# A chunked linear-recurrence scan laid out on 64x64 tiles of the array, with the solve's product in the bank of the state sum

## The chip, the cores and the metric

The kernel runs on one core of a Trainium2 chip. The metric is the device time of one execution in microseconds. Everything is fp32; on TensorE an fp32 matmul is two instructions in the trace (fp32r products aside).

## The reference

Two layers run over two batches with the same weights: a prompt of 256 tokens and a sample of 1024, 1280 tokens of width 1024 in all. Layer 0 mixes tokens by RWKV-7 in both directions, layer 1 by neighbourhood attention; each is followed by a squared-ReLU MLP. The change is in layer 0, whose core is this recurrence for 16 heads of 64, once forwards and once backwards:

```python
    def step(S, inp):
        r_t, w_t, k_t, v_t, a_t, b_t = inp
        sa = jnp.einsum('bhvk,bhk->bhv', S, a_t)
        S = S * w_t[:, :, None, :] + sa[..., None] * b_t[:, :, None, :] + v_t[..., None] * k_t[:, :, None, :]
        return S, jnp.einsum('bhvk,bhk->bhv', S, r_t)
...
        y = y + _wkv_scan(rf, _heads(decay), k_d, vf, -kk, kk * iclr, reverse=(d == 1))
        bonus = bonus + jnp.sum(rf * k_d * r_k, axis=-1, keepdims=True)
...
    y = ((y - mu) * lax.rsqrt(var + GN_EPS)).reshape(B, T, C) * lnx_g + lnx_b
    y = y + (bonus * vf).reshape(B, T, C)
```

## The kernel before

Tokens go in chunks of L = 64; heads go in pairs, m = 0 to 7, two heads filling P = 128 partitions (e = 0, 1 for the upper and lower 64). Within a chunk the recurrence is closed with a triangular system, so that each chunk is some matrix products with the 64x64 state S of each head.

**Stages.** The projections and LoRA products come first; then the operands of the scan are prepared per head pair and direction (`prep_open` and what follows it) and stored to DRAM as `ar_d` (a and r) and `bk_d` (b and k), and the bonus sums r*k_d*r_k are taken with one matmul per 128 tokens (L699, bps). Then the scan, the output projection, the MLP, attention and the second MLP.

**The scan** is ten jobs of 16 chunk steps and two directions: job 0 and 1 take the prompt (four head pairs with four chunks each), jobs 2 to 9 one head pair of the sample. The order of instructions on PE, DVE (VectorE), ACT (ScalarE) and POOL is written out by hand: `at(t, f)` gives each piece a time in steps, and the pieces are issued in the order of those times (`scan_until`); each engine runs its instructions in that order. DMA issues are SyncE's and ACT's.

A job's side work is spread over the steps before and beside it. In each of eight groups (direction d, four chunks) there are: `prod`, the product of b and a, r (L812, aps), masked into zb by DVE (L814); its store, and the reload as `mt` for the triangular solves, which DVE does in 31 pairs of rank-one operations (L857, L859) on 32x32 blocks; `merge1` and `merge2`, which join two 32-blocks with 32x32 matmuls (L903, L921) and two ACT copies; `kprod`, k with a, r (L953, kps), copied by ACT (L956) and masked by POOL (L958) into zk; `ktr`, the transpose of b, k (L967, lps, L970) into lt. PSUM tiles of these come from rotating buffers with the tag aps.

**A step** (`scan_step`) is one direction of one chunk, for both heads of the pair in 128x128 tiles with zeros off the diagonal: s0 w = zk times v (L1012); s1 adds S times ar (L1023) and ACT copies two 64x64 parts to u (L1027); s2 the solve, us = Q times u (L1032), copied by ACT to hv (L1034) and u2 (L1041); s3 the state sum, us = lt times hv (L1046), and DVE's update S = us*D + sd (L1054), where sd = S*D is POOL's (L1016); s4 w += zb times u2 (L1060), whose lower half is the chunk's y, copied by ACT (L1063) or added by DVE (L1065). The two directions are half a step apart.

`scan_post` normalises y per job in two halves (L1116 to L1163), transposes it (L1168) and stores it to z_d.

Of the kernel before, what the change touches and what calls it, by code (L numbers as in the profile page):

```python
# [23 lines left out]
NEG = -1e30  # L24
L2_EPS = 1e-24
# [3 lines left out]
V_QG, V_KG = 136, 137  # L29
NVEC = 138  # L30
# [18 lines left out]
class Trunk:  # L49
    def __init__(self, ctx, tc, a):  # L50
# [16 lines left out]
        self.dall = self.cp.tile([P, 8, 2, 20], F32, name="dall")  # L67
        self.bonus = self.cp.tile([P, 10, NH], F32, name="bonus")
# [33 lines left out]
    def l0_proj(self):  # L102
# [10 lines left out]
        W = 1283  # L113

# [400 lines left out]
    def prep_open(self, bctx):  # L515
        nc, tc, a = self.nc, self.tc, self.a
        self.ar_d = self.dram("ar_d", [8, 2, P, 20, P])
        self.bk_d = self.dram("bk_d", [8, 2, P, 20, P])
# [117 lines left out]
    def prep_products(self, U, h, i):  # L636
# [7 lines left out]
        if "ar" not in u:  # L644
            for nm in ("ar", "bk"):
                u[nm] = pk.tile([P, 8, P], F32, name=nm, tag=nm)
            u["kd"] = pk.tile([P, 512], F32, name="kd", tag=f"kd{d}", bufs=2)
            u["st"] = [(self.ar_d[m, d, :, ch0:ch0 + nch, :], u["ar"][:, :nch, :]), (self.bk_d[m, d, :, ch0:ch0 + nch, :], u["bk"][:, :nch, :])]
        ar, bk, kd = u["ar"], u["bk"], u["kd"][:, :w]
        if i == 0:  # L650
            nc.vector.tensor_tensor(out=ar[:, :nch, 64:128], in0=c3(r), in1=ec[:, :nch, 1 - d:65 - d], op=ALU.mult)
# [4 lines left out]
        elif i == 3:  # L656
            nc.vector.tensor_tensor(out=bk[:, :nch, 64:128], in0=c3(kd), in1=emc, op=ALU.mult)
        elif i == 4:
            nc.vector.scalar_tensor_tensor(out=tha, in0=tha, scalar=1.0, in1=kk, op0=ALU.add, op1=ALU.mult)
        elif i == 5:  # L660
            nc.vector.scalar_tensor_tensor(out=ar[:, :nch, 0:64], in0=c3(kk), scalar=-1.0, in1=ec[:, :nch, d:64 + d], op0=ALU.mult, op1=ALU.mult)
        elif i == 6:
            nc.vector.scalar_tensor_tensor(out=bk[:, :nch, 0:64], in0=c3(tha), scalar=0.5, in1=emc, op0=ALU.mult, op1=ALU.mult)
# [25 lines left out]
    def prep_bonus(self, U, h, step):  # L689
# [6 lines left out]
        elif step == 1:  # L696
            u["pb"] = self.ppn.tile([P, 8], F32, name="bps", tag="bps")
            for b in range(nb):
                nc.tensor.matmul(u["pb"][:, 2 * b:2 * b + 2], u["kd"][:, b * P:(b + 1) * P], self.blk, start=True, stop=True)  # L699
        else:  # L700
            nc.vector.tensor_copy(self.bonus[:, c0 // P:c0 // P + nb, 2 * m:2 * m + 2], u["pb"][:, :2 * nb].rearrange("p (b h) -> p b h", h=2))
# [6 lines left out]
    def scan_begin(self):  # L708
# [8 lines left out]
        self.r_hv, self.r_v2, self.r_q = ([[er.tile(shape, F32, name=name + "0")], 0] for name, shape in  # L717
                                          (("hv", [P, 16, P]), ("v2", [P, 16, P]), ("qq", [P, 16, 2, 64])))
        self.r_bb, self.r_ar, self.r_zb = ([[er.tile([P, 4, P], F32, name=f"{name}{i}") for i in range(n)], 0] for name, n in
                                           (("bb", 3), ("ar", 10), ("zb", 10)))  # L720
        for t in self.r_bb[0]:
            nc.gpsimd.memset(t, 0.0)
# [17 lines left out]
    def scan(self):  # L740
        nc, tc, pool = self.nc, self.tc, self.spool
        rp = self.rp = pool("rp", 1)
        fx = pool("fx", 1)

        def grow(r, pl, name, shape, n=1):
            r[0] += [pl.tile(shape, F32, name=f"{name}{len(r[0]) + i}") for i in range(n)]
        grow(self.r_hv, fx, "hv", [P, 16, P])
        grow(self.r_v2, fx, "v2", [P, 16, P])
        grow(self.r_q, fx, "qq", [P, 16, 2, 64])
        grow(self.r_ar, rp, "ar", [P, 4, P], 10)  # L750
        grow(self.r_zb, rp, "zb", [P, 4, P], 10)
        self.r_bk, self.r_u2, self.r_u1, self.r_s = [[], 0], [[], 0], [[], 0], [[], 0]
        grow(self.r_bk, fx, "bdk", [P, 4, P], 2)
        self.sp = pool("sp", 4)
# [3 lines left out]
        self.pbank = [self.pw.tile([P, 2, P], F32, name=f"us{d}") for d in range(2)]  # L758
        for r, nm, n in ((self.r_u2, "u2", 4), (self.r_u1, "u1", 3), (self.r_s, "S", 4)):
            grow(r, fx, nm, [P, P], n)  # L760
        for r in (self.r_bk, self.r_v2, self.r_u2, self.r_u1, self.r_s, self.r_q):
            for t in r[0]:
                nc.gpsimd.memset(t, 0.0)
# [13 lines left out]
    def scan_job(self, j):  # L777
# [4 lines left out]
        J = {"ar": {}, "zb": {}, "zk": {}, "lt": {}}  # L782
        order = [(0, 0), (1, 3), (0, 1), (1, 2), (0, 2), (1, 1), (0, 3), (1, 0)]


        T0 = -34.0

        def first(J=J):
            J["dd"] = [self.dsc.tile([16, 2, 64, 64], F32, name="dd", tag="dd") for _ in range(2)]
        at(T0, first, min(j + 1, 3))  # L790
        for n, (d, g) in enumerate(order):
            m, c0 = grp[g]
            t = T0 + 2 * n
            E = 1 if j == 0 else 2 if j == 1 and n < 2 else 3

            def load(d=d, g=g, m=m, c0=c0):
                ar = self.nxt(self.r_ar)
                nc.sync.dma_start(ar, self.ar_d[m, d, :, c0:c0 + 4, :])
                bb = self.nxt(self.r_bb)
                for e in range(2):  # L800
                    es = slice(64 * e, 64 * e + 64)
                    nc.sync.dma_start(bb[es, :, es], self.bk_d[m, d, es, c0:c0 + 4, 0:64])
                J["ar"][d, g], J["bb", d, g] = ar, bb

            def prod(c, d=d, g=g):
                ar, bb = J["ar"][d, g], J["bb", d, g]
                if c == 0:
                    J["zb"][d, g] = self.nxt(self.r_zb)
                    J["pa"] = self.pa.tile([P, 4, P], F32, name="aps", tag="aps")
                ps = J["pa"]  # L810
                if c < 4:
                    nc.tensor.matmul(ps[:, c, :], bb[:, c, :], ar[:, c, :], start=True, stop=True)  # L812
                if c == 4:
                    nc.vector.tensor_tensor(out=J["zb"][d, g], in0=ps, in1=self.mask[d].unsqueeze(1).to_broadcast([P, 4, P]), op=ALU.mult)  # L814

            def store(d=d, g=g, j=j):
                nc.sync.dma_start(J["dd"][d].rearrange("c e s t -> (e s) c t")[:, 4 * g:4 * g + 4, :], J["zb"][d, g][:, :, 0:64])
            at(t - (2.4 if j else 5.0), load, E)
            for c, dt in enumerate((0.05, 0.07, 0.22, 0.25, 0.38)):
                at(t + dt, lambda c=c, f=prod: f(c), E)  # L820
            at(t + 1.0, store, E)


        T1 = T0 + (15.2 if j else 16.13)

# [11 lines left out]
        at(T1, mload, 1 if j == 0 else 3)  # L837
# [4 lines left out]
        for i in range(4):  # L842
            at(T1 + (1.6 + 0.17 * i if j else 0.912 + 0.1 * i), lambda i=i: mtr(i), 1 if j == 0 else 3)
        T2 = T1 + (2.77 if j else 2.359)
        T3, load = T2, 0.0
        for jj in range(31, 0, -1):
# [13 lines left out]
            at(T3, rank1, 1 if j == 0 else 3)  # L860
            load += 400 + 2 * jj * (32 - jj)
            if load > 877.08:
# [11 lines left out]
        for i in range(4):  # L874
            at(T3 + (0.17 if j else 0.1) * i, lambda i=i: qst(i), 1 if j == 0 else 3)

        def qld():
            Q = self.nxt(self.r_q)
            qx = self.rp.tile([P, 16, 32], F32, name="qx", tag="qx", bufs=2)
            J["Q"], J["qx"] = Q, qx  # L880
# [1080 lines left out]
```

## Time and profile before

| | us |
|---|---|
| median of 3 runs | 4312.45 (4303.99 to 4316.88) |
| the profiled execution | 4314.01 |
| its span | 4312.1 |
| scan loop, 768.6 to 1565 | 796.4 |
| PE busy over the span | 3991.1 (93%) |
| DVE busy | 2660.7 (62%) |
| ACT busy | 1813.1 (42%) |
| POOL busy | 1426.1 (33%) |

Busy times are from one profiled execution. A row of a group of instructions reads: line, engine, operation, output tile<-inputs, for a matmul the rows*columns of the array that it uses, shapes, count | busy us, mean ns of one | idle time of the engine before them, and what ended it. PEld is the load of the weights, which overlaps PE. A row of a stretch of time gives its length, the busy time and count of PE, PEld, DVE, ACT and POOL, then the clock granted to PE (1.00 is full), the busy share of the DMA engines and GB/s. A row of the timeline begins with the start and the length.

### The profile page before, as it was taken

Reading aid. Unit: us, or ns where it says so; the run is one execution under the profiler, and the core shown is the slowest. Engines: PE = TensorE matmul, PEld = TensorE weight load, DVE = VectorE, ACT = ScalarE, POOL = GpSimd, SP = SyncE. Lnnn points to the kernel's source line nnn. Section 1 sums busy time; section 2 is a strip of 40 time slices with the busy share of each in tenths; the row PEclk is TensorE's granted clock in tenths of the full one; section 3 lists DMA queues with packets and bytes.
Section 4 is the critical chain, followed back from the end, with each engine's and each line's share of the span. In section 5 each row is a group of like instructions: output and inputs, shape, how many; then the busy total and the mean of one; then the engine's idle time right before and its main releaser. Section 6 shows DMA issues by size and latency. Waiting matters only on the chain.

```text
span 4312.1 us, 69598 instructions
## 1 busy us (share of the span) xinstructions
PE 3991.1 (93%) x25060; PEld 3342.6 (78%) x25060; DVE 2660.7 (62%) x5390; ACT 1813.1 (42%) x4803; POOL 1426.1 (33%) x1498
## 2 busy tenths in 40 slices
PE   7888878888998879999999998999998999999999
PEld 4665668777777758888888888877676888888888
DVE  7889963577787654755555555166665655555555
ACT  6766641677777753111111123355554311111111
POOL 5440001234444443422222234144444432222222
PEclk9997879899999989999999999999998999999999
DMA  3335565566666434111111104333335211111111
GB/s 120 81 107 198 196 201 144 141 157 155 153 151 153 108 97 133 38 39 36 40 35 40 40 31 152 117 72 77 78 70 161 65 40 40 40 35 39 35 40 59
DMA packets 484537, 400.25 MB, mean 93 GB/s; under 512 B 289216, under 2 KB 392864, under 8 KB 484192
## 3 DMA queue, kind: packets, MB, share of 16 engines
q1 hardware_dynamic: 447968, 328.56, 28.1%
q10 hardware_dynamic: 34416, 61.35, 3.9%
q0 software_dynamic: 1808, 5.90, 0.4%
q8 instruction: 197, 3.23, 0.3%
q14 instruction: 148, 1.21, 0.1%
HBM read 285.66 MB, written 121.24 MB: 94 GB/s over the span
## 4 chain that ended last, share of the span: by engine, by line
PE 69%; DVE 14%; ACT 6%; DMA 5%; issue 4%; POOL 2%; SPq 1%; ACTq 0%; DVEq 0%; POOLq 0%
PE ps L97 17%; PE ps L99 16%; PE ps L98 16%; PE w L1060 2%; PE us L1032 2%; PE kps L953 1%; PE aps L812 1%; PE vps L503 1%; PE vps L505 1%; PE vps L504 1%; PE op L1876 1%; PE us L1046 1%; PE w L1012 1%; DVE S L1054 1%; ACT u L1041 1%
## 5 line engine op out<-in xcount | busy, mean ns | idle before, releaser
L1433 DVE TENSOR_TENSOR x<-ps,x 128x256 f32<-128x256 f32 x1488 | 814.1, 595 | 628.3 <-PE ps L99 628.0
L97 PE MATMUL ps<-ah,whi 128*128 128x512 f32 (+1 forms) x2304 | 843.1, 366 | 5.0 <-ACT whi L91 4.2
L99 PE MATMUL ps<-ah,wlo 128*128 128x512 f32 (+1 forms) x2304 | 824.0, 358 | 2.1 <-POOL wlo L92 2.0
L98 PE MATMUL ps<-al,whi 128*128 128x512 f32 (+1 forms) x2304 | 823.5, 357 | 2.6 <-POOL al L1323 2.6
L92 POOL TENSOR_TENSOR wlo<-raw,whi 128x1024 fp32r<-128x1024 f32 (+1 forms) x178 | 390.5, 2194 | 851.9 <-ACT whi L91 807.8
L97 PE MATMUL ps<-hh,whi 128*128 128x512 f32 (+1 forms) x1536 | 546.9, 356 | 13.8 <-DVE x L1433 13.8
L99 PE MATMUL ps<-hh,wlo 128*128 128x512 f32 (+1 forms) x1536 | 545.9, 355 | 0.0
L98 PE MATMUL ps<-hl,whi 128*128 128x512 f32 (+1 forms) x1536 | 545.2, 355 | 0.0
L97 PEld LDWEIGHTS ps<-ah,whi 128*128 128x128 f32 x2304 | 438.8, 190 | 80.2 <-issue 13.1
L91 ACT CAST whi<-raw 128x1024 fp32r<-128x1024 f32 (+1 forms) x206 | 200.7, 975 | 696.5 <-PE ps L98 630.6
L99 PEld LDWEIGHTS ps<-ah,wlo 128*128 128x128 f32 x2304 | 437.8, 190 | 67.8 <-POOL wlo L92 2.9
L98 PEld LDWEIGHTS ps<-al,whi 128*128 128x128 f32 x2304 | 438.5, 190 | 63.0 <-POOL al L1323 2.9
L1412 POOL TENSOR_TENSOR rl<-rl 128x512 f32<-128x512 f32 (+1 forms) x192 | 174.3, 908 | 500.6 <-PE ps L99 458.3
L97 PEld LDWEIGHTS ps<-hh,whi 128*128 128x128 f32 x1536 | 291.4, 190 | 57.4 <-DVE x L1433 16.8
L1411 ACT ACTIVATE rl<-ps 128x512 f32<-128x512 f32 (+1 forms) x192 | 100.8, 525 | 546.4 <-PE ps L99 546.4
L98 PEld LDWEIGHTS ps<-hl,whi 128*128 128x128 f32 x1536 | 291.4, 190 | 41.0
L99 PEld LDWEIGHTS ps<-hh,wlo 128*128 128x128 f32 x1536 | 291.4, 190 | 41.1
L1414 ACT CAST hh<-rl 128x512 fp32r<-128x512 f32 (+1 forms) x192 | 105.5, 549 | 321.0 <-POOL rl L1412 320.9
L1054 DVE SCALAR_TENSOR_TENSOR S<-us,dall,sd 64x64 f32<-64x64 f32 x512 | 145.0, 283 | 126.4 <-PE us L1046 115.7
L1415 DVE TENSOR_TENSOR hl<-rl,hh 128x512 fp32r<-128x512 f32 (+1 forms) x192 | 119.4, 622 | 151.6 <-ACT hh L1414 151.1
L1016 POOL TENSOR_TENSOR sd<-S,dall 128x128 f32<-128x128 f32 x256 | 122.5, 480 | 258.2 <-DVE S L1054 174.8
L1060 PE MATMUL w<-u,zb 128*128 128x128 f32 x640 | 158.2, 330 | 47.0 <-ACT u L1041 44.8
(310 smaller groups left out, 8222.4 us busy)
## 6 DMA issues: line engine op xcount, KB each, us to landing
raw<-in_w_down_dram SPq DMA_DIRECT2D x64, 512.0 KB, 3.5
raw<-in_w_up_dram SPq DMA_DIRECT2D x64, 512.0 KB, 3.4
ar<-ar_d SPq DMA_DIRECT2D x80, 256.0 KB, 3.4
bk<-bk_d SPq DMA_DIRECT2D x80, 256.0 KB, 3.5
ar_d<-ar ACTq DMA_DIRECT2D x32, 512.0 KB, 2.7
bk_d<-bk ACTq DMA_DIRECT2D x32, 512.0 KB
bs<-tab SPq DMA_DIRECT2D x128, 96.0 KB, 3.9
v_d<-vt ACTq DMA_DIRECT2D x80, 128.0 KB, 4.0
```

The costliest lines, as they stand in the source:

```text
L91: nc.scalar.copy(hi[:, cs], raw)
L92: lo_eng.tensor_tensor(out=lo[:, cs], in0=raw, in1=hi[:, cs].bitcast(F32), op=ALU.subtract)
L97: mm(ps, sh, mh, start=first, stop=False)
L98: mm(ps, sh, ml, start=False, stop=False)
L99: mm(ps, sl, mh, start=False, stop=last)
L1016: nc.gpsimd.tensor_tensor(out=R["sd"], in0=st["S"], in1=self.dall[:, m, d, ch:ch + 1].to_broadcast([P, P]), op=ALU.mult)
L1054: nc.vector.scalar_tensor_tensor(out=S2[es, es], in0=sn[es, es], scalar=D, in1=R["sd"][es, es], op0=ALU.mult, op1=ALU.add)
L1060: nc.tensor.matmul(w, J["zb"][d, g][:, c, :], R["u2"], start=False, stop=True, skip_group_check=True)
L1412: nc.gpsimd.tensor_tensor(out=r[:, :n], in0=r[:, :n], in1=r[:, :n], op=ALU.mult)
L1414: nc.scalar.copy(hh[:, :n], r[:, :n])
L1415: nc.vector.tensor_tensor(out=hl[:, :n], in0=r[:, :n], in1=hh[:, :n].bitcast(F32), op=ALU.subtract)
L1433: nc.vector.tensor_tensor(out=xv, in0=ps[:, :n], in1=xv, op=ALU.add)
```

## The change

All products of the scan are written on 64x64 tiles of the array. HALVES names the two pairs of partition halves: a matmul with the operands on es (64 rows) and the output on es or eo (64 columns) is one tile, so that a product of both heads is two matmuls on different tiles, and a, r, b, k and v lie in tiles of 64 columns without zeros off the diagonal. Both directions are one chain: one set of ACT copies per step serves both. The state sum is in PSUM as identity times S, plus lk times v, plus lb times u, and ACT scales it by the decay when it copies it back; DVE's update and POOL's sd are gone. The banks are b_a (for w's first half), two b_y and two b_s; U, the solve's product, is in columns 128 to 255 of the b_s bank whose first 128 columns take the state sum. Three rotating buffers (pa) serve the side work, where DVE masks zk straight from PSUM. The output transposes and `ktr` are matmuls with the identity. Operands are stored in DRAM by kind and token, the affine part of the normalisation goes to an ACT activation after the transpose, and the bonus sums become 64x64 matmuls per chunk and head. The budget of rank-one work per half step goes from 877.08 to 930.

```diff
+HALVES = ((slice(0, 64), slice(64, 128)), (slice(64, 128), slice(0, 64)))
...
-            for b in range(nb):
-                nc.tensor.matmul(u["pb"][:, 2 * b:2 * b + 2], u["kd"][:, b * P:(b + 1) * P], self.blk, start=True, stop=True)
+            for c in range(2 * nb):
+                for es, eo in HALVES:
+                    nc.tensor.matmul(u["pb"][eo, c:c + 1], u["kd"][es, c * L:(c + 1) * L], self.one[es], start=True, stop=True)
...
+        self.b_a = self.pw.tile([P, 512], F32, name="ba")
+        self.b_y, self.b_s = ([self.pw.tile([P, 512], F32, name=f"{nm}{i}") for i in range(2)] for nm in ("by", "bs"))
...
+            def prod(h, d=d, g=g):
+                if h == 0:
+                    J["pa"] = w4(self.pa.tile([P, 512], F32, name="aps", tag="aps"))
+                if h < 2:
+                    for c in (2 * h, 2 * h + 1):
+                        for es, eo in HALVES:
+                            mm(J["pa"][es, c], J["bb", d, g][es, c], J["aa", d, g][es, c], start=True, stop=True)
...
-            if load > 877.08:
+            if load > 930.0:
                 T3, load = T3 + 0.5, 0.0
...
+            def kprod(h, d=d, g=g):
...
+                    for c in (2 * h, 2 * h + 1):
+                        for es, eo in HALVES:
+                            mm(J["pb"][es, c], bb[es, c], rr[es, c], start=True, stop=True)
+                            mm(J["pk"][eo, c, 0:64], kk[es, c], aa[es, c], start=True, stop=True)
+                        for es, eo in HALVES:
+                            mm(J["pk"][eo, c, 64:128], kk[es, c], rr[es, c], start=True, stop=True)
+                elif h == 2:
+                    zk = J["zk", d, g] = self.rp.tile([P, 4, P], F32, name="zk", tag="zk", bufs=5)
+                    nc.vector.tensor_tensor(out=zk, in0=J["pk"], in1=b4(self.mask[d], P), op=ALU.mult)
...
         def s0():
+            A, Y, sn, U = banks()
+            for d, g, c, cc, m, ch in dirs:
+                zk, v, yd = J["zk", d, g], J["v"], 1 - d if second else d
+                for es, eo in HALVES:
+                    mm(A[es, d], zk[eo, c, 0:64], v[eo, cc], d == 0, new)
+                    mm(Y[eo, yd], zk[eo, c, 64:128], v[eo, cc], d == 0, False)
+                if not end:
+                    for es, eo in HALVES:
+                        mm(sn[es, d], J["lk", d, g][eo, c], v[eo, cc], d == 0, False)
...
+            for d, g, c, cc, m, ch in dirs:
+                yd = 1 - d if second else d
+                for es, eo in HALVES:
+                    mm(A[es, d], J["aa", d, g][es, c], S[es, d], False, True)
+                    mm(Y[eo, yd], J["rr", d, g][es, c], S[es, d], False, False)
+            if not end:
+                for d in range(2):
+                    for es, eo in HALVES:
+                        mm(sn[es, d], self.ident[es, es], S[es, d], False, False)
+
+        def s1c():
...
+            nc.scalar.copy(R["up"], A)
 
         def s2():
+            A, Y, sn, U = banks()
+            for d, g, c, cc, m, ch in dirs:
+                for es, eo in HALVES:
+                    mm(U[es, d], J["Q"][es, cc, d], R["up"][es, d], end and d == 0, True)
 
         def s2c():
...
+            nc.scalar.copy(R["u"], U)
 
         def s3():
+            A, Y, sn, U = banks()
+            for d, g, c, cc, m, ch in dirs:
+                yd = 1 - d if second else d
+                for es, eo in HALVES:
+                    if not end:
+                        mm(sn[es, d], J["lb", d, g][es, c], R["u"][es, d], False, True)
+                    mm(Y[eo, yd], J["zr", d, g][es, c], R["u"][es, d], False, True)
+
+        def s3c():
+            A, Y, sn, U = banks()
+            S = st["S"] = self.sp.tile([P, 2, 64], F32, name="S", tag="S", bufs=3)
+            for d, g, c, cc, m, ch in dirs:
+                nc.scalar.activation(S[:, d], sn[:, d], AF.Copy, scale=self.dall[:, m, d, ch:ch + 1])
```

PE, in the middle of a job before the change: one half step and its side work, a matmul per row. us is the solve's product or the state sum, w the chunk's own bank, yps and qps the merges.

```order
L1046 MATMUL us_7181<-hv_7146,lt 128x128 [waits Activation_49]
L1060 MATMUL w<-u_7182,zb_6197 128x128 [waits Activation_49]
L1012 MATMUL w<-v_7147,zk 128x128 [waits PE_49]
L1032 MATMUL us_7181<-u_7188,qq_7148 128x128 [waits DVE_49,Activation_49]
L1023 MATMUL w<-S_7191,ar_6187 128x128
L953 MATMUL kps<-ar_7150,bdk_7170 128x128 [waits DMAHW2_49,DMAHW1_49]
L953 MATMUL kps<-ar_7150,bdk_7170 128x128
```

PE, in the middle of a job after it: part of one step of both directions, from the end of s1 over the product of another job and s2 to the next step's s0. ba, by and bs are the banks, cst the identity.

```order
L993 MATMUL ba<-S,aa_6420 64x64
L993 MATMUL by_7443<-S,rr 64x64
L993 MATMUL bs_7445<-S,cst 64x64 x4
L812 MATMUL aps<-aa_7405,bb_7417 64x64 [waits DMAHW7_49,DMAHW5_49,DVE_49]
L812 MATMUL aps<-aa_7405,bb_7417 64x64 x7
L993 MATMUL bs_7445<-up,qq_7392 64x64 [waits Activation_49]
L993 MATMUL bs_7445<-up,qq_7392 64x64 x3
L993 MATMUL ba<-vv_7391,zk 64x64
L993 MATMUL by_7442<-vv_7391,zk 64x64
```

The five matmuls of 128x128 of a half step have become 36 of 64x64 for both directions, and the side work between them is 64x64 as well; the waits on DVE's update of S are gone, one on DVE's emptying of aps (L812) is there.

DVE, in the middle of the rank-one solves before the change. q<-q,tmp and tmp<-mt,q are one rank-one pair, S the update of the state.

```order
L857 TENSOR_TENSOR tmp<-mt,q 128x255 [waits DVE_49]
L859 TENSOR_TENSOR q<-q,tmp 128x17x15 [waits DVE_49]
L1054 SCALAR_TENSOR_TENSOR S_7192<-us_7180,dall,sd 64x64 [waits PE_49,Pool_49]
L1054 SCALAR_TENSOR_TENSOR S_7192<-us_7180,dall,sd 64x64
L814 TENSOR_TENSOR zb_7164<-aps,cst 128x512 [waits PE_49]
L857 TENSOR_TENSOR tmp<-mt,q 128x256 [waits DVE_49]
L859 TENSOR_TENSOR q<-q,tmp 128x16x16 [waits DVE_49]
```

The same place after it:

```order
L858 TENSOR_TENSOR tmp<-mt,q 128x255 [waits DVE_49]
L860 TENSOR_TENSOR q<-q,tmp 128x17x15 [waits DVE_49]
L858 TENSOR_TENSOR tmp<-mt,q 128x256 [waits DVE_49]
L860 TENSOR_TENSOR q<-q,tmp 128x16x16 [waits DVE_49]
L1113 TENSOR_REDUCE va<-ysq 128x8 [waits Activation_49]
L1120 TENSOR_SCALAR rqx<-va 128x8 [waits DVE_49]
L858 TENSOR_TENSOR tmp<-mt,q 128x255
L860 TENSOR_TENSOR q<-q,tmp 128x15x17 [waits DVE_49]
L858 TENSOR_TENSOR tmp<-mt,q 128x252 [waits DVE_49]
L860 TENSOR_TENSOR q<-q,tmp 128x14x18 [waits DVE_49]
L948 TENSOR_TENSOR zk<-kps,cst 128x512 [waits PE_49]
L951 TENSOR_TENSOR zr<-bps,cst 128x256
```

Two pairs stand where one stood, with the output's normalisation (va) and the masking of zk and zr among them.

More of the change, by code (lines that the diff above doesn't have):

```diff
@@ L113, in l0_proj @@
         W = 1283
+        kp = self.sctx.enter_context(tc.tile_pool(name="kp", bufs=1))
+        self.dall = kp.tile([P, 8, 2, 20], F32, name="dall")
+        self.bonus = kp.tile([P, 12, 20], F32, name="bonus")
         mixctx = ExitStack()
@@ L805, in prod @@
[L805 to L824, printed above, removed]
+                J["aa", d, g], J["bb", d, g] = self.nxt(self.r_aa), self.nxt(self.r_bb)
@@ L1176, in scan_post, with p4 @@
-            if last:
-                when = (-4.0 if tail else -0.2, -0.186, 0.474, -0.5 if tail else 1.327, 1.601, -0.4 if tail else 1.982, 1.843, 2.252, 2.253, 2.254, 3.521, 4.15, 4.563, 5.809, 5.819)
-            else:
-                tr0 = 21.72 + 2 * half + 8 * (left > 1)
-                when = (0.05, 0.0, 0.3, 1.5, 0.55, 1.75, 0.85, 1.1, 1.2, 1.4, 1.6, 2.1, 2.6, tr0 - t0, tr0 + 0.48 - t0)
-            for dt, f in zip(when, (ld, p1, p2, p3a, p2b, p3b, p2c, lambda f=p3: f(0), lambda f=p3: f(1), lambda f=p3: f(2), p4, p4b, p5, tr, trc)):
+            def p4(st=st, y=y):
+                nc.vector.tensor_tensor(out=y(), in0=y(), in1=each(four(st["rq"][1])), op=ALU.mult)
```

452 lines of the change are left out of this document (195 added, 257 removed).

## The prediction

> **What bounds the kernel now.** I first read the page, then the busy times by stage, then the groups of the scan loop, then a few microseconds of its timeline.
>
> ```profile
> span 4312.1 us, 69598 instructions
> PE 3991.1 (93%) x25060; PEld 3342.6 (78%) x25060; DVE 2660.7 (62%) x5390; ACT 1813.1 (42%) x4803; POOL 1426.1 (33%) x1498
> core 0: us, PE busy (x) PEld busy (x) DVE busy (x) ACT busy (x) POOL busy (x), PEclk, DMA share, GB/s
> 300.00:735.00 435.00, 371.88 (x1959) 294.12 (x1958) 310.24 (x573) 217.90 (x464) 13.14 (x23) 0.83 0.56 187
> 735.00:768.60 33.60, 20.39 (x129) 18.74 (x130) 4.27 (x7) 6.74 (x15) 11.58 (x25) 0.60 0.81 181
> 768.60:1565.00 796.40, 701.07 (x7072) 610.51 (x7071) 576.41 (x1563) 584.86 (x2309) 343.98 (x575) 0.97 0.58 138
> 1565.00:1606.00 41.00, 24.93 (x112) 19.53 (x113) 30.32 (x48) 15.31 (x29) 20.75 (x16) 0.76 0.48 146
> 1606.00:4312.10 2706.10, 2622.95 (x14561) 2220.43 (x14559) 1482.69 (x2813) 778.15 (x1555) 886.69 (x711) 0.98 0.21 62
> ```
>
> The change touches four of these stages: the preparation of the scan's operands (300 to 735), the ramp (735 to 768.6), the scan loop and its tail (to 1606). What follows is untouched. The loop holds ten jobs of 16 steps in 796.4 us, 79.6 us a job and 4.98 a step; the PE there has work in flight for 88% of the time and its clock is almost full (0.97).
>
> ```profile
> L1060 PE MATMUL w<-u,zb 128*128 128x128 f32 x639 | 157.9, 330 | 47.0 <-ACT u L1041 44.8 <-DVE S L1054 0.4 <-DVE tmp L857 0.4
> L1054 DVE SCALAR_TENSOR_TENSOR S<-us,dall,sd 64x64 f32<-64x64 f32 x512 | 145.0, 283 | 126.4 <-PE us L1046 115.7 <-POOL sd L1016 2.1 <-POOL sgl L1290 1.2
> L1041 ACT COPY u<-us 64x64 f32<-64x64 f32 x640 | 132.4, 207 | 10.6
> L859 DVE TENSOR_TENSOR q<-q,tmp 128x60 f32<-128x60 f32 (+14 forms) x261 | 113.1, 433 | 9.0
> L857 DVE TENSOR_TENSOR tmp<-mt,q 128x87 f32<-128x87 f32 (+14 forms) x260 | 102.5, 394 | 6.8
> L1034 ACT COPY hv<-us 64x128 f32<-64x128 f32 x320 | 83.5, 261 | 154.9 <-PE us L1032 148.4
> L1065 DVE TENSOR_TENSOR y<-w,y 64x128 f32<-64x128 f32 x159 | 46.5, 292 | 37.6 <-PE w L1060 34.1
> L814 DVE TENSOR_TENSOR zb<-aps,cst 128x512 f32<-128x512 f32 x63 | 43.6, 691 | 7.1 <-PE aps L812 5.4
> ...
> L1120 DVE TENSOR_TENSOR y<-y,mu 128x512 f32<-128x512 f32 x19 | 14.8, 781 | 0.3
> ...
> L1116 DVE TENSOR_REDUCE mu<-y 128x8 f32<-128x512 f32 x19 | 12.9, 678 | 0.1
> ...
> 1100.51 0.49 PE L1060 MATMUL w<-u,zb 128*128 128x128 f32 x2
> ...
> 1100.83 0.39 PE L1012 MATMUL w<-v,zk 128*128 128x128 f32 x2
> 1100.86 0.42 DVE L857 TENSOR_TENSOR tmp<-mt,q 128x252 f32<-128x252 f32 x1
> ...
> 1102.69 0.49 PE L1060 MATMUL w<-u,zb 128*128 128x128 f32 x2 [0.36 <-ACT u L1041]
> ...
> 1103.58 0.53 PEld L812 LDWEIGHTS aps<-ar,bb 128*128 128x128 f32 x4
> 1103.69 0.61 PE L812 MATMUL aps<-ar,bb 128*128 128x128 f32 x4
> ```
>
> A half step (one direction) takes 2.19 us, 1100.51 to 1102.69: it is the chain of matmul, ScalarE copy, matmul, copy, matmul, VectorE update of S (283 ns), with the two directions interleaved in one array. The waits named, ACT u and PE us, are links of that chain. An fp32 matmul is two instructions; four of them last 0.61 us and two 0.39, so each further one costs (0.61-0.39)/2, about 0.11 us, and the last one's tail about 0.2.
>
> **The change part by part.** *The scan step.* Both directions go through one chain, on 64x64 tiles: 12 matmuls for S times a, r and the identity, a copy of 128x128, 4 for the solve, a copy, 8 for the state sum and Y, two scaled ScalarE copies; 12 more (the v terms) fill. The VectorE update and POOL's product are gone. The solve's product U stands in the bank of the state sum, behind it; the next step uses the other of two such banks, so this adds no wait that the chain does not have anyway, and SyncE issues four loads per group of chunks in place of six: nothing for both. Copies I take at 261 ns (L1034's row, also 128 elements long) and 207 (L1041's), 0.94 us together. The price of a 64-wide tile stands outside the loop:
>
> ```profile
> 2955.18 0.45 PE L1845 MATMUL op<-s,vs 128*64 128x64 f32 x8
> ...
> 3273.35 0.69 PE L1845 MATMUL op<-s,vs 128*64 128x64 f32 x8
> ```
>
> Eight instructions on two column tiles: warm 0.45 us. With a tail of 0.22, as above, four instructions on each tile leave (0.45-0.22)/4 = 58 ns apiece, if the tiles run side by side, and that is half of the 0.11 found for a full-width one. The second row is the same work at half clock: (0.69-0.26)/4 = 107 ns. I take four 64x64 tiles as concurrent too, an estimate: there is no such row. On the busiest tile a step then has 8 + 8 + 4 + 4 = 24 instructions. The fillers of a job (products, their transposes now as products with the identity, merges, output transposes) are 576 matmuls: kprod 128 instructions on its busiest tile, the other five kinds (prod, ktr, two merges, output) 64 each, 448 together. A job: 16 x 24 + 448 = 832 instruction slots. Warm that is 832 x 0.058 = 48 us, at half clock 832 x 0.107 = 89 us. The chain, warm: three PE links, their slots (24 less the 8 that fill, 0.9 us) and a tail of 0.22 at each hand-off (0.7), and 0.94 of copies, 2.6 us. So a warm light step is about 3.1 (PE slots 24 + 28 = 52, 3.0 us), against 4.98 now.
>
> *VectorE.* The rank-one solves (31 pairs a job, 433 + 394 ns by the rows; about 21 us without the stretching beside POOL, by the 0.42 in the timeline) were one pair per half step, since a pair of middle length weighs 912 against a budget of 877; the budget is now 930, two pairs go into each half step, and the solve is squeezed into some 7.5 steps. With zk (691 ns by L814's row) and zr, za (0.42 each, by the row of 128x252) for eight groups, the y sums (0.29 each, L1065) and two output groups (four operations like L1120's, two like L1116's, some small: 4.9 us each) a job has 21 + 8 x 1.53 + 2.3 + 9.8 = 45 us of VectorE work; by their places in the changed program seven steps carry 32.5 of it, most of them 4.3 to 5.9. These wait for VectorE, because it empties the three product banks; the nine others cost it 0.4 to 2.9.
>
> So with a full clock a job is 32.5 + 9 x 3.1 = 60 to 64 us: 600 to 640 for the loop, 155 to 195 saved. All of this hangs on the clock, so I looked at where the clock changes now.
>
> ```profile
> 345.50:348.90 3.40, 3.40 (x8) 1.48 (x8) 3.37 (x7) 1.62 (x4) 0.00 (x0) 0.50 0.48 142
> 348.90:352.30 3.40, 2.46 (x3) 0.50 (x2) 1.55 (x3) 2.78 (x8) 0.00 (x0) 0.50 0.78 308
> 362.60:366.00 3.40, 3.40 (x16) 3.05 (x16) 2.06 (x7) 2.16 (x5) 0.00 (x0) 0.50 0.47 169
> 366.00:369.40 3.40, 3.40 (x15) 1.42 (x12) 3.33 (x7) 2.58 (x5) 0.00 (x0) 1.00 0.24 90
> 758.50:761.90 3.40, 3.40 (x44) 3.11 (x43) 0.69 (x1) 0.75 (x3) 0.00 (x0) 0.50 0.74 131
> 761.90:765.30 3.40, 2.39 (x12) 2.09 (x10) 0.00 (x0) 1.79 (x6) 0.35 (x1) 0.50 0.89 193
> 1154.50:1157.90 3.40, 2.47 (x44) 1.81 (x42) 2.96 (x7) 1.94 (x7) 2.91 (x6) 1.00 0.88 144
> 1157.90:1161.30 3.40, 3.40 (x17) 3.22 (x16) 1.46 (x4) 1.63 (x8) 2.34 (x6) 0.50 0.86 223
> 1161.30:1164.70 3.40, 3.25 (x27) 2.97 (x27) 0.88 (x4) 2.46 (x10) 0.80 (x2) 1.00 0.72 164
> ...
> L607 PE MATMUL l<-tw,wa 64*128 64x512 f32 x4 | 2.1, 1135 | 0.0
> L607 PE MATMUL l<-ta,wa 64*128 64x512 f32 x2 | 1.9, 1054 | 0.0
> ...
> L921 PE MATMUL qps<-qq,yt 32*32 32x32 f32 x16 | 0.7, 237 | 0.0
> L903 PE MATMUL yps<-qx,zb 32*32 32x32 f32 x16 | 0.6, 239 | 0.0
> ```
>
> These are 3.4-us stretches on the clock's own grid. A stretch full of 128-row matmuls at half clock (362.6) is followed by a full clock. A stretch just as busy (345.5, 3.40 of 3.40), but of 64-row matmuls (the L607 rows), is not, nor is 758.5, busy throughout, where 32 of the instructions are 32x32 (the L921 and L903 rows). And at 1154.5 the PE was busy 2.47 of 3.40 us with 44 instructions, many of them small tiles, and lost the clock for a stretch. So what counts is not that the PE is busy but how much of the array is: I read that half clock ends only after a stretch with about 0.75 of the array's cycles used, and full clock after one below about 0.37. [...]
>
> Counted by area, a 64x64 tile is a quarter of the array. At half clock a job's 2304 instructions use 2304/4 x 0.107 = 62 us of array out of 89: 0.69, below 0.75. Warm, a VectorE-bound step of 5.5 us uses 144/4 x 0.058 = 2.1 us, 0.38, at the edge of losing the clock; and the loop starts cold (0.60 in the ramp). So the loop falls to half clock and is held there, PE-bound: 89 us a job. Less the products of the first two jobs, which lie in the ramp, and what their steps without a state before or after them leave out, the ten come to 846 us; with 3 to 8% of gaps at the hand-offs 870 to 915, and I take 888, +92.
>
> *The rest.* Bonus sums of the preparation:
>
> ```profile
> L699 PE MATMUL bps<-cst,kd 128*128 128x2 f32 x160 | 30.8, 311 | 31.9 <-DVE bonus L701 31.9
> ```
>
> 160 instructions become 640 of 64x64, half of them side by side: 320 slots of 0.058 to 0.107 us, 19 to 34, against 160 of 0.11 to 0.21, 18 to 34: nothing by rates, something by changes of tile shape between 128-wide matmuls, for which there is no row; 0 to 15, I take 8, since the PE is busy 372 of 435 us there. Ramp and tail move fewer, longer packets and drop the affine pass: -5 each (0 to -8). The sum: 4314.0 + 92 + 8 - 5 - 5 = 4404 for the profiled execution (span 4312.1, 4314.0 with its launch), which stands 1.6 above the median: 4402.
>
> **The rivals.** *The clock stays full*, because a pair of diagonal tiles feeds all 128 rows, and the count goes by rows fed. For it: the L607 rows show that rows matter; against it: the 32x32 stretch at 758.5 stayed cold, though pairs of tiles on different rows, and the products beside them, filled it. Price: loop 620, -176, sum 4314 - 176 - 2 - 1.6, 4134; with VectorE bursts that take more than counted, up to 4210; I write 4155. It ends on the other side; it decides from a count of 0.75 in a cold stretch, which I put at 0.69, so it is near. [...]
>
> *A mixture*: light stretches lift the clock, VectorE-bound ones lose it. A job is 7 x 5.8 + 9 x 3.3 = 70 to 80 us, the loop 700 to 800; 4215 to 4315, say 4260.
>
> *The tiles do not run four at a time* (only pairs do, as in the L1845 row). The change then doesn't do what it says: scan and mixed fillers double, 4.2 us of slots a warm step and 8 cold; total from 4340, warm, to 4800, cold. The two directions and the crossed tiles write to different banks, which speaks for four.
>
> **How the numbers follow.** Half clock 0.53, at 4402 with its own range 4335 to 4450; full clock 0.32 at 4155; mixture 0.11 at 4260, nearly all faster; only pairs 0.04, slower. About 0.3% (13 us) is what a measurement of this kernel can tell from no change. Faster: 0.32 + 0.09 = 0.41 less a hundredth or two for rounding at the edge, 0.40; same 0.03; slower 0.57. The predicted time is the likeliest case, 4402. For 8 in 10 the range takes in half clock, the mixture and the upper half of full clock: 4145 to 4450.
>
> **What would show it.** In the changed kernel's loop: granted clock 0.5 to 0.6 and PE busy over 90% (right), or 0.9 and more with VectorE-bound steps of 5 to 6 us and light ones near 3 (first rival); a clock that alternates once a job (mixture). The rate of a tile's instructions within one step: 107 ns at half clock, 58 at full, on four tiles at once; if the second tile pair starts only when the first ends, the third rival. A loop of 870 to 915 us is the forecast; below 796 it is wrong.

## The result and the profile after

The changed kernel took 4193.16 us (median of 4, 4189.98 to 4198.98) against 4312.86 of the kernel before: a ratio of 0.9727, 95% interval [0.9707, 0.9746], by this ratio 118 us, 2.7%, faster. The forecast was 4402, slower, on a clock held at half. The measured time lies inside the stated range of 4145 to 4450, but on the other side of the kernel before, in the first rival's place: 4193 where I wrote 4155 with an upper end of 4210.

The page of the profile after, its first two lines and the row of TensorE's instruction fetches, and the same row of the page before (packets, MB, share of the DMA engines):

```profile
span 4189.1 us, 97599 instructions
PE 3808.8 (91%) x40500; PEld 3201.6 (76%) x40500; DVE 2466.7 (59%) x4870; ACT 1537.4 (37%) x3671; POOL 1139.3 (27%) x998
q8 instruction: 318, 5.21, 0.5%
...
q8 instruction: 197, 3.23, 0.3%
```

318 packets of 5.21 MB are 16 KB each; PE and PEld together are 81,000 instructions, and 81000/318 is 255. Before, 50,120/197 is 254. So one such packet is a block of 256 TensorE instructions, weight loads counted (the streams below give it exactly: 10,752 instructions in 42 packets). The prediction has nothing of that row.

The stages by time. In the first two rows of before the cut is the first and the last matmul of a scan step, in the five of after likewise (756.7 and 1451.1):

```profile
763.70:1561.90 798.20, 702.48 (x7075) 612.09 (x7075) 576.71 (x1562) 584.84 (x2303) 346.69 (x580) 0.97 0.58 139
1561.90:4312.10 2750.20, 2649.35 (x14681) 2241.00 (x14679) 1514.21 (x2862) 795.77 (x1592) 908.18 (x727) 0.98 0.22 64
...
300.00:723.00 423.00, 359.34 (x2450) 281.75 (x2449) 306.41 (x571) 219.53 (x465) 12.76 (x20) 0.84 0.57 185
723.00:756.70 33.70, 18.68 (x421) 16.83 (x421) 8.02 (x21) 1.95 (x6) 4.58 (x6) 0.75 0.77 187
756.70:1451.10 694.40, 537.53 (x21614) 488.39 (x21611) 390.36 (x1040) 314.97 (x1187) 71.78 (x102) 0.95 0.45 116
1451.10:1480.00 28.90, 20.24 (x203) 18.49 (x200) 15.02 (x29) 9.85 (x20) 9.55 (x8) 0.73 0.48 152
1480.00:4189.10 2709.10, 2623.21 (x14595) 2216.99 (x14593) 1491.82 (x2825) 782.88 (x1563) 891.16 (x714) 0.98 0.20 63
```

The loop went from 798.2 to 694.4 (-103.8); its start came 7.0 earlier (763.7 to 756.7), of which 1.1 is the preparation (the last bonus sum begins at 630.1, before at 631.2) and 5.9 the ramp; what follows went from 2750.2 to 2738.0 (-12.2). Together -123.0, the difference of the two spans. The loop's clock is 0.95, not a half. PE has work in flight for 537.5 of 694.4 us, 77%, where it had 88%.

What the loop waits for shows in its timeline (PE alone, a stretch of light steps; a product of 16 instructions, and the two instructions behind a pause):

```profile
1070.03 0.68 PE L812 MATMUL aps<-aa,bb 64*64 64x64 f32 x16
...
1073.08 0.21 PE L959 MATMUL lbps<-cst,bb 64*64 64x64 f32 x1 [1.50 <-issue]
1077.20 0.27 PE L993 MATMUL bs<-vv,lk 64*64 64x64 f32 x2 [1.22 <-issue]
```

The product runs at the price of the prediction: 8 instructions on each of two tiles, 8 x 0.058 + 0.22 = 0.68. But at 1073.08 and at 1077.20 PE stood 1.50 and 1.22 us "for issue": nothing that the profile shows was missing. Counted in the trace, there are 255 instructions between these two pauses and 253 to 255 between the next ones (1081.3, 1085.4, 1088.9). Over the loop, the pauses of PE above 0.3 us add up to 139.6 us, counted in the trace. By what ended them, 73.6 us are "issue", 40.6 ScalarE and 25.3 VectorE. Of the 139.6, 83.8 us (99 pauses, for 170 blocks) end 1.1 to 1.75 us after a block of instructions landed, all the "issue" ones among them. That interval is 16% of the 4.07 us between two blocks, so chance would put some 22 us there. In the loop before, 4.3 of 81 us end so.

### The profile page after: what moved, and what is told of

It is laid out like the page before. It is cut to its first block, busy times and chain, and to the rows that moved or that the text cites. A ratio compares the mean times of both kernels' runs of the same rounds, so it can differ in the third digit from the quotient of the medians.

```text
span 4189.1 us, 97599 instructions
## 1 busy us (share of the span) xinstructions
PE 3808.8 (91%) x40500; PEld 3201.6 (76%) x40500; DVE 2466.7 (59%) x4870; ACT 1537.4 (37%) x3671; POOL 1139.3 (27%) x998
## 3 DMA queue, kind: packets, MB, share of 16 engines
q8 instruction: 318, 5.21, 0.5%
## 4 chain that ended last, share of the span: by engine, by line
PE 70%; DVE 15%; issue 5%; ACT 4%; DMA 4%; POOL 1%; SPq 1%; ACTq 0%; DVEq 0%; POOLq 0%
PE ps L96 17%; PE ps L97 17%; PE ps L98 17%; PE bs L993 2%; DVE q L860 1%; PE ba L993 1%; PE vps L506 1%; DVE tmp L858 1%; PE vps L507 1%; PE vps L508 1%; PE by L993 1%; PE op L1849 1%; PE aps L812 1%; PE pt L1791 1%; DVE mu L187 1%
## 5 line engine op out<-in xcount | busy, mean ns | idle before, releaser
L96 PE MATMUL ps<-hh,whi 128*128 128x512 f32 (+1 forms) x1536 | 547.4, 356 | 12.4 <-DVE x L1406 12.2
L1784 POOL TENSOR_TENSOR s<-s,mx 128x384 f32<-128x384 f32 (+1 forms) x154 | 116.8, 769 | 207.6 <-DVE mx L1783 136.3
L1068 DVE TENSOR_TENSOR y<-by,y 128x128 f32<-128x128 f32 x80 | 24.7, 309 | 164.7 <-PE by L993 164.6
L1782 ACT ACTIVATE s<-s,mx 128x384 f32<-128x384 f32 (+1 forms) x154 | 87.1, 567 | 79.0 <-DVE mx L1781 77.6
```

The costliest lines, as they stand in the source:

```text
L96: mm(ps, sh, mh, start=first, stop=False)
L1784: nc.gpsimd.tensor_tensor(out=s[:, :nk], in0=s[:, :nk], in1=mx[:, 2:3].to_broadcast([P, nk]), op=ALU.mult)
```

## The experiments

**The clock.** A program with TensorE patterns alone, which leaves the computation out:

```python
FORMS = {"one": [(lo, lo, 0)], "diag": [(lo, lo, 0), (hi, hi, 0)], "cols": [(lo, lo, 0), (lo, hi, 1)],
         "four": [(lo, lo, 0), (hi, hi, 0), (lo, hi, 1), (hi, lo, 1)], "row": [(lo, al, 0)], "col": [(al, lo, 0)], ...}
for r, c, bank in FORMS[f]:
    nc.tensor.matmul(ps[bank][c], w[r, c], mv[r], start=True, stop=True, skip_group_check=True)
```

> Leaves out the whole computation: it only runs TensorE patterns of 512-column fp32 matmuls, each after some 8 us of idling, so that each starts at half clock. In order: 128x128; one 64x64 tile; two 64x64 tiles on the diagonal; two on the same rows; four; one 64x128; one 128x64; then a full clock made by 128x128 and after it one 64x64 tile, a diagonal pair, one 32x32 tile, a pair on the same rows, 13.7 us each without gaps. If the count goes by area (step of the prediction): 128x128 and four tiles reach full clock, pairs (0.5), the 64x128 and the 128x64 (0.5) and the single tile (0.25) stay at half; after a full clock the single tile (0.25) and the 32x32 tile (0.06) lose it, pairs keep it. If it goes by rows fed (first rival): the diagonal pair, the four and the 128x64 reach full clock, the single tile, the pair on the same rows and the 64x128 (0.5) do not; after a full clock the single tile (0.5) keeps it, the 32x32 tile (0.25) loses it. If any busy PE counts, all reach it and all keep it.

By stretches of time (length, PE, PEld, DVE, POOL, then the granted clock, DMA share, GB/s), in this order: one tile; diagonal pair, its begin and its rest; pair on the same rows; four, begin and rest; 64x128; 128x64, begin and rest; and after a full clock one tile, a diagonal pair, one 32x32 tile, a pair on the same rows.

```profile
39.40:53.30 13.90, 13.89 (x16) 3.46 (x16) 0.00 (x0) 0.00 (x0) 0.50 0.00 0
58.90:62.70 3.80, 3.80 (x10) 1.18 (x12) 0.00 (x0) 0.00 (x0) 0.51 0.00 0
62.70:67.80 5.10, 5.10 (x24) 1.37 (x20) 0.00 (x0) 0.00 (x0) 1.00 0.00 0
73.40:87.30 13.90, 13.90 (x32) 3.54 (x32) 0.00 (x0) 0.00 (x0) 0.50 0.01 1
92.90:96.80 3.90, 3.89 (x20) 1.29 (x24) 0.00 (x0) 0.00 (x0) 0.50 0.00 0
96.80:101.90 5.10, 5.10 (x48) 1.43 (x40) 0.00 (x0) 0.00 (x0) 1.00 0.00 0
107.50:121.60 14.10, 14.02 (x16) 5.16 (x16) 0.01 (x1) 0.00 (x0) 0.50 0.00 0
127.10:130.90 3.80, 3.79 (x5) 1.22 (x6) 0.00 (x0) 0.00 (x0) 0.50 0.00 0
130.90:136.10 5.20, 5.17 (x12) 1.37 (x10) 0.00 (x0) 0.00 (x0) 1.00 0.00 0
148.50:162.40 13.90, 13.86 (x32) 4.09 (x32) 0.00 (x0) 0.00 (x0) 1.00 0.00 0
175.50:189.20 13.70, 13.67 (x64) 4.19 (x60) 0.00 (x0) 0.00 (x0) 1.00 0.00 0
206.00:226.10 20.10, 20.10 (x24) 3.70 (x22) 0.00 (x0) 0.00 (x0) 0.50 0.00 0
240.20:253.40 13.20, 13.20 (x62) 4.05 (x58) 0.00 (x0) 0.00 (x0) 1.00 0.00 0
```

All of it is as the count by rows has it. A diagonal pair, half of the array's area but all 128 rows, lifted the clock from 0.51 to 1.00 after 3.8 us, and so did the 128x64, from 0.50; the 64x128 and the pair on the same rows have the same area and half of the rows and stayed at 0.50 for 14 us of uninterrupted work. A single 64x64 tile (half the rows) did not lift the clock (0.50 for 13.9 us) but kept it (1.00 for 13.9 us); a 32x32 tile (a quarter) lost it (0.50 in the row of 206.0).

In the scan loop the four crossing tiles and the diagonal pairs feed both halves of the rows. Six stretches of the changed kernel, cut on the grid of its clock's changes (counted in the trace, they lie whole multiples of 3.41 us apart):

```profile
746.50:749.90 3.40, 3.11 (x88) 2.87 (x84) 1.35 (x3) 0.00 (x0) 0.00 (x0) 0.50 0.99 178
753.40:756.80 3.40, 1.05 (x35) 1.05 (x37) 2.33 (x8) 0.09 (x1) 0.88 (x2) 1.00 0.78 221
756.80:760.20 3.40, 3.14 (x92) 3.01 (x90) 2.89 (x9) 1.93 (x6) 0.00 (x0) 0.50 0.91 260
777.20:780.60 3.40, 1.65 (x66) 1.46 (x59) 3.19 (x10) 1.24 (x6) 0.00 (x0) 1.00 0.28 83
780.60:784.10 3.50, 3.50 (x116) 3.50 (x112) 2.42 (x10) 1.19 (x5) 0.72 (x2) 0.51 0.16 42
821.60:825.00 3.40, 1.93 (x61) 1.71 (x56) 1.12 (x4) 1.91 (x6) 0.00 (x0) 1.00 0.47 128
```

After 746.5 and after 756.8 (PE in flight for 3.1 of 3.4 us, though only some 0.6 of the area-time by my sum over the instructions) the clock is full in the next stretch (0.99 and 1.00); 753.4 and 777.2, thinly filled (1.05 and 1.65 us), are followed by half a clock (0.50 at 756.8, 0.51 at 780.6), 821.6 (1.93 us) is not (1.00). The loop has few such stretches: 0.95 over all.

**The pace.** Three one-line changes of the changed kernel, run on the same chip in the same rounds. The wide identity:

```diff
-                for d in range(2):
-                    for es, eo in HALVES:
-                        mm(sn[es, d], self.ident[es, es], S[es, d], False, False)
+                for es, eo in HALVES:
+                    mm(sn[es], self.ident[es, es], S[es], False, False)
```

> The identity times S of each step as two matmuls of 128 columns in place of four of 64: the same columns streamed, 8 TensorE instructions (weight loads counted) less in 128 steps, 1024 in all. Theory F (the loop runs at the pace at which blocks of 256 TensorE instructions are fetched, 4.1 us each): 4 blocks less, -16 us, 0.4% (4193 to 4177). Theory S (the pace is that of the array and the chain): the stream is the same, 0 to -3 us. Theory D (VectorE's heavy steps): 0.

The split identity:

```diff
-                    for es, eo in HALVES:
-                        mm(sn[es, d], self.ident[es, es], S[es, d], False, False)
+                    for q0 in (0, 32):
+                        for es, eo in HALVES:
+                            mm(sn[es, d, q0:q0 + 32], self.ident[es, es], S[es, d, q0:q0 + 32], False, False)
```

> The identity times S of each step as eight matmuls of 32 columns in place of four of 64: the same columns streamed, 16 TensorE instructions more in 128 steps, 2048 in all, 8 blocks of 256. Theory F: +33 us (4193 to 4226). Theory S: four slots of 58 ns on the busiest tile become eight of about 32 (the 32x32 rate), +0.03 us a step, +3 us. Theory D: 0 to +3.

The budget of the rank-one work:

```diff
-            if load > 930.0:
+            if load > 877.08:
```

> The budget of rank-one work per half step put back to 877.08: the pairs of middle length go one to a half step, the solve spreads over 9.5 steps in place of 7.5. TensorE's instructions are the same in number. Theory D: the heavy steps (4.9 us a step over seven of them by VectorE's load) come down to about 4.3, 4 us a job, -30 to -45 us. Theory F: the job's 18 blocks at 4.1 us remain, 0 to -10 us. Theory S: 0 to -20.

Measured against the kernel before (4315.49): wide 4202.81, 0.9743 [0.9724, 0.9762]; split 4239.06, 0.9829 [0.981, 0.9847]; 877.08 4205.0, 0.9752 [0.9733, 0.9771]. Split against wide, 12 blocks apart, is 36 us, 3.0 a block; theory F had 49, theory S 3 to 6. But this does not decide between them. In the trace of the split kernel the instructions of 32 columns start 58 ns apart on a tile, as those of 64 do, and not about 32: from the first to the last start of a step's identity it is 394 ns by the median, against 188 in the changed kernel and 125 in the wide one. With the last instruction's own slot that is 0.45 against 0.23 us a step for split against wide, 128 times, so the array alone may take up to 28 of the 36 us. The wide identity, against 4193, seemed to gain nothing. Nor did the spread solve, where theory D had asked for 30 to 45 us. These two compare runs of different sets, and a difference of 0.4% needs the changed kernel in the same set; the next set had it.

> The changed kernel as it is, on the same chip and beside the same runs as the three that follow, so that they can be compared with it: 0.9727 of the kernel before, as measured.

a and r in one tile, k times both in one matmul:

```diff
-                            mm(J["pk"][eo, c, 0:64], kk[es, c], aa[es, c], start=True, stop=True)
-                        for es, eo in HALVES:
-                            mm(J["pk"][eo, c, 64:128], kk[es, c], rr[es, c], start=True, stop=True)
+                            mm(J["pk"][eo, c], kk[es, c], J["ar", d, g][es, c], start=True, stop=True)
```

> a and r of a group lie in one tile, and k times a and k times r become one matmul of 128 columns: 64 matmuls less a job, 256 TensorE instructions, a block of 256 a job, 10 in all; the columns streamed are the same. Theory F (a block takes at least some 4 us to be fetched, so the light steps wait for it): up to -41 us, and at least -10 if only the waiting of about 1 us at each block's start is saved. Theory S (array and chain set the pace): 0 to -3. The run with the wide identity, which should have given -16 by F, gave nothing, so F at its full size is already in doubt.

b times both as well (the matmuls for bps fall away; to make room the gate's raw buffers go from 7 to 4, bv from 2 to 1, and the last job makes its bv later):

```diff
-                            mm(J["pa"][es, c], J["bb", d, g][es, c], J["aa", d, g][es, c], start=True, stop=True)
+                            mm(J["pa"][es, c], J["bb", d, g][es, c], J["ar", d, g][es, c], start=True, stop=True)
...
-                            mm(J["pb"][es, c], bb[es, c], rr[es, c], start=True, stop=True)
...
-                    nc.vector.tensor_tensor(out=J["za", d, g], in0=J["pa"], in1=b4(self.mask[d][:, 0:64], 64), op=ALU.mult)
+                    nc.vector.tensor_tensor(out=z, in0=J["pa"], in1=b4(self.mask[d], P), op=ALU.mult)
```

> As the one before, and b times a and b times r also become one matmul of 128 columns, early, with one VectorE mask of 128x512 in place of two of 128x256: 128 matmuls less a job in all, 512 TensorE instructions, 2 blocks of 18; VectorE 1.2 us a job less, one PSUM buffer a group less. Theory F: up to -82 us, at least -20. Theory S: 0 to -5. Theory D (VectorE's bursts and the three PSUM buffers): -10 to -25, from the load and the buffer.

And with the wide identity:

> As the one before, with the wide identity as well: 6144 TensorE instructions less over the loop, 24 blocks of 169. Theory F: up to -98 us, at least -24. Theory S: 0 to -8. Theory D: -10 to -25.

The instruction rows of the four pages, in this order (the changed kernel again, k wide, b wide, all wide):

```profile
q8 instruction: 318, 5.21, 0.5%
...
q8 instruction: 308, 5.05, 0.5%
...
q8 instruction: 298, 4.88, 0.5%
...
q8 instruction: 294, 4.82, 0.5%
```

| kernel | blocks | time, us | ratio to before (4315.82) | loop of its profile, us | pauses behind a landing in it, us |
|---|---|---|---|---|---|
| changed, again | 318 | 4215.12 | 0.977 [0.9757, 0.9783] | 711.5 | 103.5 |
| k wide | 308 | 4186.66 | 0.9705 [0.9689, 0.9722] | 688.9 | 75.3 |
| b wide too | 298 | 4169.0 | 0.9662 [0.9649, 0.9676] | 656.6 | 52.1 |
| all wide | 294 | 4157.37 | 0.9637 [0.9624, 0.965] | 644.9 | 36.6 |

The same columns stream through the array in all four, and each block less is worth 2.3 to 2.9 us (28 for 10, 46 for 20, 58 for 24). That is theory F at 0.56 to 0.7 of a block's 4.1 us; theory S, with 0 to 8 us in all, is out. The wide identity, from the third row to the fourth, is worth 11.6 us here, 2.9 a block. The last two columns come from the traces, one profile each, the pauses added up as above (above 0.3 us, ending 1.1 to 1.75 us after a landing): the loop fell by 67 us and these pauses by 67. The b-wide step also saves VectorE work and a buffer, so its 20 blocks are not quite pure; the two others are. The changed kernel itself gave 4215 here and 4193 in the first set, with the kernel before the same to 0.1%; its loop was 711.5 and 694.4. Why it differs between sets stays open (the later sets ran on different chips); within a set it does not move the comparison.

**The price by itself.** Streams on all four tiles with nothing to wait for, the computation left out:

```python
for n, k in ((64, 192), (32, 192), (128, 192), (256, 96)):
    for _ in range(k):
        for r, c, bank in FORMS["four"]:
            nc.tensor.matmul(ps[bank][c, 0:n], w[r, c], mv[r, 0:n], start=True, stop=True, skip_group_check=True)
```

> Leaves out the whole computation: it only runs streams of 64x64 fp32 matmuls on all four tiles in turn, with nothing to wait for and no transfers beside them: 768 matmuls of 64 columns, 768 of 32, 768 of 128 (each 12 blocks of 256 TensorE instructions), 384 of 256 columns (6 blocks), with some 8 us of idling between. By the array (S) a block is 16 rounds of 4 matmuls at two instructions of 58 ns each: 1.9 us at 64 columns, 1.0 at 32, 3.4 at 128, 6.8 at 256. By the fetch (F) a block takes no less than some 3.5 us (2.5 from a landing to the next fetch, 1.1 for the fetch), whatever the columns: 3.5 at 32 and at 64, 3.5 to 4 at 128, 6.8 at 256, with a pause every 256 instructions in the first two.

Its timeline in the stream of 64 columns, PE alone, the whole stream of 32 columns as a stretch of time, and the groups by shape:

```profile
41.26 2.09 PE L1887 MATMUL ps<-mv,w 64*64 64x64 f32 x128 [1.36 <-issue]
45.26 2.09 PE L1887 MATMUL ps<-mv,w 64*64 64x64 f32 x128 [1.91 <-issue]
48.99 2.09 PE L1887 MATMUL ps<-mv,w 64*64 64x64 f32 x128 [1.64 <-issue]
...
73.20:115.50 42.30, 41.66 (x1518) 41.03 (x1519) 0.00 (x0) 0.00 (x0) 0.50 0.02 4
...
L1887 PE MATMUL ps<-mv,w 64*64 64x256 f32 x768 | 44.2, 392 | 5.1 <-DVE mv L1891 5.1
L1887 PE MATMUL ps<-mv,w 64*64 64x128 f32 x1536 | 44.0, 275 | 5.0 <-DVE mv L1891 5.0
L1887 PE MATMUL ps<-mv,w 64*64 64x32 f32 x1536 | 42.5, 292 | 5.8 <-DVE mv L1891 5.1 <-issue 0.4
L1887 PE MATMUL ps<-mv,w 64*64 64x64 f32 x1536 | 27.0, 229 | 41.1 <-DVE mv L1883 24.8 <-issue 16.3
```

This is the mechanism with everything else taken away. 128 matmul instructions (with 128 loads, one block) run in 2.09 us, of which 0.22 is the tail: 32 on each tile at 58 ns (32 x 0.058 + 0.22 = 2.08), so four tiles do run at once, and the weight loads beside them cost nothing more. Then nothing for 1.4 to 1.9 us; the next block begins 3.5 to 4.0 us after the last. By the starts of the instruction packets a block takes 3.65 us at 64 columns, 3.6 at 128, where the array needs 3.4 by the estimate above and the pauses are all but gone, and 6.9 at 256, where the array sets the pace (6.8 by the estimate). So I take some 3.6 us a block as a floor at 64 columns, an estimate from these streams, nearly twice the array's time; in no run do two of these packets start less than 3.27 us apart. The stream of 32 columns ran at half clock, at 3.66 us a block with hardly a pause: its instructions start 107 ns apart on each tile, the half-clock price of 64 columns, and it says nothing of the floor. It says something of the clock: all four tiles were in flight for 41.7 of 42.3 us, and the clock stayed at 0.50. So rows in flight are not enough. That the array is fed for only half of each 107 ns, 32 columns where 64 fit, would explain it, but no run tests that.

**What is left.** All wide, with the spread solve, and all wide again beside it:

> The kernel with all wide matmuls and the budget of rank-one work put back to 877.08. With a seventh of the blocks gone the waits on VectorE weigh more: theory D, -10 to -30 against the kernel with all wide matmuls; theory F with what is left of its waits, 0 to -5.

> The kernel with all wide matmuls again, beside the one before: 0.964 of the kernel before, as measured.

4154.68, 0.9626 [0.9604, 0.9647], and 4154.68, 0.9627 [0.9612, 0.9642], against 4316.28. Where the rank-one pairs lie makes no difference that shows in the time, with the shorter stream of instructions side by side and with the longer one across sets. The profiles show why spreading the solve need not help: in the run with 877.08 PE waits 42 us for VectorE and ScalarE, in pauses above 0.3 us, where the changed kernel waits 66, but 113 us for "issue" in place of 74 (57 and 94 in the changed kernel again). What one wait gives up the other takes; with one profile each that is a hint. Theory D by itself is out. All wide is the fastest of the kernels run, 3.7% under the kernel before. U in another bank was not tried, so what its place is worth stays open.

## Why the prediction was right and wrong

- **What bounds the kernel now** was not tested by itself. The change replaced the chain of a half step and its array time together, and no run separates the small tiles from the joint chain of both directions; which of them brought the gain is not shown.
- **The clock: wrong, and this made the forecast.** The step that failed is "Counted by area, a 64x64 tile is a quarter of the array". The count goes by rows fed: e1's diagonal pair at 1.00 against the pair on the same rows at 0.50, with equal area. The 0.75 and 0.37 of that count were my reading of the prediction's rows, and no run bears them out: the diagonal pair lifted the clock with half of the area, and one tile kept it (1.00) with a quarter. The rows that I had (64-row matmuls, 345.5) could not tell area from rows, and the 32x32 stretch at 758.5, which I put against the rows, may fit them as well, since a 32x32 tile feeds a quarter of them; that is argued, not shown. The 0.69 that was held against 0.75 was also too low: 832 slots add up the busiest tile of each phase, but it is not always the same tile. One on the diagonal takes 20 of a step's 72 instructions and a crossed one 16, not 24. In the cold stretch at 780.6 the array has up to 116 x 0.107 / 4 = 3.1 of 3.5 us, 0.89, so even the count by area, with its 0.75, would have lifted the clock there. With the clock at 0.95 the 92 us more became 104 less.
- **Array prices right.** 58 ns an instruction and tile and a tail of 0.22: the L812 row (0.68, two tiles). Four tiles at once: the streams (2.09 for a block). The third rival, only pairs, is out.
- **The first rival's price: the clock right, but 155 to 195 saved in the loop against 104 measured.** The term left out is the supply of instructions. The change makes 43,225 TensorE instructions of 14,150 in the loop (21614 + 21611 against 7075 + 7075), 169 blocks of 256 against 55. A whole job is 18 blocks, and at the 3.65 us of the streams 18 x 3.65 = 66 us is a floor, by estimate, that my 60 to 64 lay under; over the loop, which lacks some of the first jobs' work, the floor is 169 x 3.65 = 617 us, as long as the 600 to 640 that I had added up. The measured 694 us are 4.1 a block. The two limits do not simply overlap: 694.4 less the 83.8 us of pauses behind a landing is 611, an estimate of the loop without them. Before, 798/55 = 14.5 us a block, far from the floor. That 4193 lies under the rival's upper end of 4210 is luck, since that end was kept for longer VectorE bursts.
- **VectorE's heavy steps: not the limit by themselves.** Rank-one operations took 353 and 349 ns, 22 us a job, as the 21 of the prediction had it (before, by the trace, one of L859 with 128x255 took 424 ns alone and 647 by the mean beside POOL), but spreading them gave nothing:

```profile
L860 DVE TENSOR_TENSOR q<-q,tmp 128x135 f32<-128x135 f32 (+14 forms) x259 | 91.4, 353 | 8.9
L858 DVE TENSOR_TENSOR tmp<-mt,q 128x135 f32<-128x135 f32 (+14 forms) x259 | 90.4, 349 | 5.1
```

- **The copies** of the chain took 265 and 266 ns (forecast 261); the scaled ones 312 by the mean (forecast 207, from a row half as high):

```profile
L1060 ACT ACTIVATE S<-bs,dall 128x64 f32<-128x64 f32 x288 | 74.8, 312 | 53.5 <-PE by L993 48.7 <-PE bs L993 4.4
L1045 ACT COPY u<-bs 128x128 f32<-128x128 f32 x160 | 42.5, 266 | 105.9 <-PE bs L993 104.6 <-PE by L993 0.6
L1034 ACT COPY up<-ba 128x128 f32<-128x128 f32 x160 | 42.4, 265 | 86.1 <-PE ba L993 81.1 <-PE by L993 3.5
```

- **The rest.** Preparation: -1.1 against +8; the 640 small bonus matmuls cost nothing, changes of tile shape included. Ramp -5.9 against -5. Tail and what follows -12.2 against -5.

## What to carry to other kernels

Before small matmuls replace large ones, divide the engine's instructions, weight loads included, by 256 and compare with the time: a stretch that would need a block in under some 4 us waits for its instructions (4.1 us a block here, 14.5 before). One matmul of 128 columns in place of two of 64 then halves the instructions for the same columns. A timeline in which the PE pauses "for issue" about every 256 instructions is the sign. For the clock, count the rows that are fed, not the area: put small tiles on different rows at the same time (1.00 in e1, against 0.50 for the pair on the same rows with the same area), and keep them fed (0.50 after a stretch with 1.05 us in flight of 3.4); with 32 columns a matmul that was not enough here (0.50 for 42 us).

## What was not expected of the hardware

- A block of 256 TensorE instructions followed the last one after 3.5 to 4.0 us, with the DMA engines 2% busy (the stream of 64 columns), and in no run after less than 3.27; the packet itself takes some 1.1 us of that, by the row of TensorE's queue in 40 us of the changed kernel's loop (1060 to 1100): 1.7% of 16 engines, 10.9 us, for 10 packets.

```profile
q8 instruction: 10, 0.16, 1.7%
```

- With 512 columns a matmul, the clock rose to 1.00 after 3.8 to 3.9 us with all 128 rows fed (diagonal pair, four tiles, 128x64) and stayed at 0.50 for 14 us with 64 rows, on 64 of the array's columns and on 128; after a full clock it stayed at 1.00 with 64 rows (13 to 14 us) and fell to 0.50 with 32 (e1). With 32 columns a matmul it did not rise (0.50) in 42 us on all rows (the streams).
- An instruction of 32 columns held a 64x64 tile as long as one of 64: 58 ns at full clock (the split identity), 107 at half (the streams).
- 64x64 matmuls with one column between 128-wide ones cost the preparation nothing that shows: its last bonus sum begins at 630.1, before at 631.2.
